# Splitting layer two's weight tiles into high and low halves in two pieces of 1024 columns

## The chip, the cores and the metric

The kernel runs on one core of one Trainium2 chip. The metric is the device time of one execution in microseconds. Three runs of the kernel before took 905.1, 906.5 and 909.17 us, with a median of 906.5 us. The profile is of one more execution.

## The reference

It is one step of a two-layer decoder trunk for 256 prompt tokens and 8 sample tokens, 264 in all, with a model width of 2048. Layer one is sliding-window attention, layer two is a gated linear recurrence (HGRN2) with 12 heads of 128 by 128 state. Each layer also has 4 memory heads, a SiLU gate as wide as the branch, one output projection, and a LayerNorm. Cut to what layer two computes:

```python
def _hgrn_branch(h, w_in, lb, norm_w, s0):
    q, f, iv, mq, g = _split(jnp.einsum('btd,de->bte', h, w_in), HG_SPLITS)
    fg = lb[None, None, :] + (1.0 - lb[None, None, :]) * jax.nn.sigmoid(f)
    qh, kh, gh, vh = silu(q), 1.0 - fg, log(fg), iv          # by heads of 128
    o, s_new = _hgrn2_chunked(qh, kh, vh, gh, s0)
    o = o * lax.rsqrt(jnp.mean(jnp.square(o), -1, keepdims=True) + RMS_EPS) * norm_w
    return o, s_new, mq, g

def _finish(h, mix, mq, g, mk, mv, w_out_i, ln_w_i, ln_b_i):
    mem_o = _mem_attend(mq, mk, mv)
    branch = jnp.concatenate([mix, mem_o], axis=-1) * jax.nn.silu(g)
    return _layer_norm(DEEPNORM_ALPHA * h + jnp.einsum('bte,ed->btd', branch, w_out_i), ln_w_i, ln_b_i)
```

## The kernel before

**A stream of tiles.** All weights and caches come through one stream of tiles of 128 rows by 2048 columns, f32 (`raw`, four buffers, loaded by SP's queue). A tile of the recurrence's state has 1024 columns. `Stream.prep` splits a tile into two f16 halves, so that f32 products can be made from f16 matmuls: line 97 has ScalarE (ACT) write the high half `hl[:, 0]`, a scaled copy; line 98 has VectorE (DVE) write the low half `hl[:, 1]`, what the copy lost. `hl` has four buffers. `Stream.parts` gives the columns of each piece: the first tile goes in four pieces, the next three in two, all others whole.

**What a tile is used for.** `proj` (line 303 to 305 by way of `passes`) multiplies a weight tile with all 264 tokens: 16 chunks of 128 rows, three matmuls for each: high by high (L303), high by the tokens' low half (L304), low by high (L305). That is 48 matmuls on TensorE (PE) for one tile. A tile of a cache or of the state needs 32 or 16 much smaller matmuls.

**The tiles of layer two**, in order: for each of six pairs of heads, two tiles for `f`, two for `hv`, two for `hq`, two of state, and for the first four pairs two for the early gates; then four for `mq`, then the memory caches (`c_mk`, four tiles, whose matmuls are named `mss`; `c_mv`, four tiles, `mso`) interleaved with the eight late gates (`g`), then the 16 tiles of the output projection (`o`).

**Work beside the stream.** The recurrence of a pair (`hg_side`) runs beside the following tiles. It makes the scores over seven levels: DVE and ACT prepare operands of level h (`prepare`: ACT high half, L1079; DVE low half, L1080; DVE's product for the next level, L1084), PE multiplies them (`hs`), and DVE masks the scores into `st` (L1111). The last level goes into `st` by ACT (L1147). Then follows a chain on PE: `pk` (transposes of the keys, L1152), `pu` (state update, L1158), `hpo` (output, L1169 to L1171) and `rms` (L1182), with steps of ACT and DVE between them. The softmax of the sample tokens over the memory keys (`mrow`, `mback`) has its own chain; it uses the same two PSUM banks (`pt`) as `pk` and `pu`, and `mso` waits for it.

**What sets the order.** The program is written unit by unit, and a scheduler puts each engine's instructions in an order of its own from that. Each engine then runs its queue strictly in that order: an instruction that waits holds all behind it.

Of the kernel before, what the change touches and what calls it, by code (L numbers as in the profile page):

```python
# [57 lines left out]
class Stream:  # L58


    def __init__(self, nc, pool, nraw, nsplit):
        self.nc, self.pool = nc, pool
        self.nraw, self.nsplit = nraw, nsplit
        self.units = []
        self.raw = {}
        self.hl = {}

    def add(self, src, fn, scale=SW, pre=None, split=True, whole=False, home=None):
        self.units.append((src, fn, scale, pre, split, split and not whole, home))
# [14 lines left out]
    def prep(self, i):  # L84
        _, _, scale, _, split, _, home = self.units[i]
        raw = self.raw[i]
        if not split:
            self.hl[i] = raw
            return
        if home:  # L90
            hl = home(i)
        else:
            hl = self.pool.tile([P, 2, 2048], F16, tag="hl", name=f"hl{i}", bufs=self.nsplit)
        for k, s in enumerate(self.parts(i)):
            if i < 4:
                self.before_split(i, k)
            hi = self.nc.scalar.activation(hl[:, 0, s], raw[:, s], AF.Copy, scale=scale)  # L97
            lo = self.nc.vector.scalar_tensor_tensor(  # L98
                hl[:, 1, s], raw[:, s], scale, hl[:, 0, s], op0=ALU.mult, op1=ALU.subtract
            )  # L100
            if i < 2:
                self.settled = hi, lo
        self.hl[i] = hl
# [31 lines left out]
def trunk_kernel(  # L135
# [42 lines left out]
    stream = Stream(nc, cp, 4, 4)  # L178
# [527 lines left out]
    def gate_unit(l, j):  # L706
        def fn(hl):
            pt = proj(hl, xhl, T, f"g{l}{j}")
            a = cp.tile([P, T], F32, tag="sil", name=f"sil{l}{j}", bufs=3)
            silu2(a, pt)  # L710
            fin[l].append((a, j))
            if len(fin[l]) >= 3:
                gate_fin(l)

        return fn
# [51 lines left out]
    def out_unit(l, i):  # L767
        def fn(hl):
            if i == 0:
                drain()  # L770
                while fin[l]:
                    gate_fin(l)
                for s in range(2):
                    acc[s] = cp.tile([P, T], F32, tag="mphl", name=f"acc{l}{s}", bufs=2)
            if l == 0 or i < NC - NSPLIT:
                out_part(l, i, hl, slice(0, T))
            else:
                held[i] = hl
                out_part(l, i, hl, slice(0, TA))
            if i == NC - 1:  # L780
                if l == 0:
                    side.append(layer_norm())
                else:
                    finish_tokens()

        return fn
# [123 lines left out]
    def wb(w, i):  # L910
        return w[i].rearrange("p c f -> p (c f)")
# [97 lines left out]
    def hq_unit(h):  # L1009
        def fn(hl):  # L1010
            p1 = H["p"]
            pt = proj(hl, xhl, T, f"hq{h}")
            if h % 2 == 0:
                cur["q"] = p1.tile([P, 2, T], F32, tag="hq", name=f"hqs{h}", bufs=2)
            silu2(cur["q"][:, h % 2], pt)
            if h % 2 == 1:
                side.append(hg_side(h // 2, cur["q"], cur["vn"], cur["fg"], cur["qk"]))

        return fn
# [31 lines left out]
    def early_gate(j):  # L1051
        def fn(hl):
            silu2(mix[:, j], proj(hl, xhl, T, f"g1{j}"))

        return fn
# [187 lines left out]
        return fn  # L1243

    state_at = {}
    for pi in range(HD // 2):
        for part, unit in (("f", f_unit), ("v", hv_unit)):
            for i in range(2):
                stream.add(wb(w_in1, NB1[part] + 2 * pi + i), unit(2 * pi + i))
        for h in (2 * pi, 2 * pi + 1):  # L1250
            stream.add(wb(w_in1, NB1["q"] + h), hq_unit(h))
            state_at[h] = len(stream.units)
            stream.add(state[pi][:, (h % 2) * TS * P : (h % 2 + 1) * TS * P], state_unit(h), SA, whole=True)
            if h < NG1:
                stream.add(wb(w_in1, NB1["g"] + h), early_gate(h))
# [9 lines left out]
    def g1(j):  # L1265
        stream.add(wb(w_in1, NB1["g"] + j), gate_unit(1, j))
# [5 lines left out]
            g1(late.popleft())  # L1272
    while late:
        g1(late.popleft())
    for i in range(NC):
        stream.add(wb(w_o[1], i), out_unit(1, i), home=hold if i >= NC - NSPLIT else None)

# [155 lines left out]
```

## Time and profile before

| what | value |
|---|---|
| runs | 905.1, 906.5, 909.17 us |
| the profiled execution's own time | 906.08 us |
| its span | 904.3 us (1.8 us lie around it) |
| PE busy | 886.6 us, 98% of the span |
| DVE busy | 701.5 us, 78% |
| ACT busy | 582.4 us, 64% |
| mean granted PE clock | 0.994 |

A matmul's end is modelled in these records, and matmuls overlap; whether PE really works is better read from the distance between their starts. Layer two's recurrence lies between about 415 and 740 us, its caches and late gates between about 730 and 800 us, and its output projection behind that.

### The profile page before, as it was taken

Reading aid. Unit: us, or ns where it says so; the run is one execution under the profiler, and the core shown is the slowest. Engines: PE = TensorE matmul, PEld = TensorE weight load, DVE = VectorE, ACT = ScalarE, POOL = GpSimd, SP = SyncE. Lnnn points to the kernel's source line nnn. Section 1 sums busy time; section 2 is a strip of 40 time slices with the busy share of each in tenths; the row PEclk is TensorE's granted clock in tenths of the full one; section 3 lists DMA queues with packets and bytes.
Section 4 is the critical chain, followed back from the end, with each engine's and each line's share of the span. In section 5 each row is a group of like instructions: output and inputs, shape, how many; then the busy total and the mean of one; then the engine's idle time right before and its main releaser. Section 6 shows DMA issues by size and latency. Waiting matters only on the chain.

```text
span 904.3 us, 21814 instructions
## 1 busy us (share of the span) xinstructions
PE 886.6 (98%) x9281; PEld 762.9 (84%) x9281; DVE 701.5 (78%) x1230; ACT 582.4 (64%) x982; POOL 34.9 (4%) x68
## 2 busy tenths in 40 slices
PE   9999999999999999999999999999999999799996
PEld 6888889678888888876888888898888888688996
DVE  6879877669886666697687887979788989678736
ACT  6767776657664444476766877777777585858415
POOL 1100010000000000002000000000000000000000
PEclk9999999999999999999999999999999999899999
DMA  9998566557785555556374655827454878456303
GB/s 340 392 353 317 188 245 209 188 208 265 262 333 192 187 192 203 207 198 214 127 292 137 216 201 174 299 101 260 160 215 164 303 283 308 172 207 244 130 2 97
DMA packets 37853, 198.67 MB, mean 220 GB/s; under 512 B 4555, under 2 KB 10732, under 8 KB 17532
## 3 DMA queue, kind: packets, MB, share of 16 engines
q1 hardware_dynamic: 33024, 181.55, 56.3%
q0 software_dynamic: 4688, 15.67, 4.6%
q8 instruction: 72, 1.18, 0.5%
q14 instruction: 25, 0.20, 0.1%
q10 hardware_dynamic: 44, 0.07, 0.0%
HBM read 180.03 MB, written 17.22 MB: 218 GB/s over the span
## 4 chain that ended last, share of the span: by engine, by line
PE 77%; DVE 8%; ACT 6%; DMA 6%; issue 3%; SPq 0%; ACTq 0%; DVEq 0%
PE o L303 5%; PE o L305 5%; PE o L304 5%; PE g L305 5%; PE g L303 5%; PE g L304 5%; DVE hl L98 4%; ACT hl L97 2%; PE hv L305 2%; PE hv L303 2%; PE hv L304 2%; DMA raw<-in_w_in 2%; PE hq L303 2%; PE hq L305 2%; PE hq L304 2%
## 5 line engine op out<-in xcount | busy, mean ns | idle before, releaser
L98 DVE SCALAR_TENSOR_TENSOR hl<-raw,hl 128x2048 f16<-128x2048 f32 (+2 forms) x168 | 358.6, 2138 | 82.0 <-ACT hl L97 81.0
L97 ACT ACTIVATE hl<-raw 128x2048 f16<-128x2048 f32 (+2 forms) x168 | 299.2, 1784 | 97.8 <-PE o L305 45.4
L305 PEld LDWEIGHTS <-hl 128*128 128x128 f16 (+2 forms) x2048 | 197.4, 98 | 31.8 <-DVE hl L98 2.9
L303 PEld LDWEIGHTS <-hl 128*128 128x128 f16 (+2 forms) x2048 | 197.3, 98 | 30.6 <-issue 2.2
L304 PEld LDWEIGHTS <-hl 128*128 128x128 f16 (+2 forms) x2048 | 197.4, 98 | 30.3 <-issue 2.2
L305 PE MATMUL g<-xhl,hl 128*128 128x264 f16 x512 | 142.0, 277 | 2.4 <-DVE hl L98 2.4
L303 PE MATMUL g<-xhl,hl 128*128 128x264 f16 x512 | 141.9, 277 | 0.0
L304 PE MATMUL g<-xhl,hl 128*128 128x264 f16 x512 | 141.9, 277 | 0.0
L303 PE MATMUL o<-mix,hl 128*128 128x264 f16 x384 | 105.4, 276 | 0.8 <-DVE xres L747 0.8
L304 PE MATMUL o<-mix,hl 128*128 128x264 f16 x384 | 105.8, 276 | 0.0
L305 PE MATMUL o<-mix,hl 128*128 128x264 f16 x384 | 105.7, 276 | 0.0
L303 PE MATMUL q<-xhl,hl 128*128 128x264 f16 x192 | 53.0, 276 | 1.0 <-DVE kst L251 1.0
L303 PE MATMUL f<-xhl,hl 128*128 128x264 f16 x192 | 52.9, 276 | 0.4 <-DVE mvhl L251 0.4
L305 PE MATMUL hv<-xhl,hl 128*128 128x264 f16 x192 | 53.0, 276 | 0.0
L303 PE MATMUL hq<-xhl,hl 128*128 128x264 f16 x192 | 53.0, 276 | 0.0
L304 PE MATMUL hq<-xhl,hl 128*128 128x264 f16 x192 | 53.0, 276 | 0.0
L305 PE MATMUL hq<-xhl,hl 128*128 128x264 f16 x192 | 53.0, 276 | 0.0
L304 PE MATMUL hv<-xhl,hl 128*128 128x264 f16 x192 | 53.0, 276 | 0.0
L303 PE MATMUL hv<-xhl,hl 128*128 128x264 f16 x192 | 53.0, 276 | 0.0
L304 PE MATMUL q<-xhl,hl 128*128 128x264 f16 x192 | 53.0, 276 | 0.0
L305 PE MATMUL q<-xhl,hl 128*128 128x264 f16 x192 | 53.0, 276 | 0.0
L304 PE MATMUL f<-xhl,hl 128*128 128x264 f16 x192 | 52.9, 276 | 0.0
(338 smaller groups left out, 1858.4 us busy)
## 6 DMA issues: line engine op xcount, KB each, us to landing
raw<-in_w_in SPq DMA_DIRECT2D x88, 1024.0 KB, 6.4
raw<-in_w_o SPq DMA_DIRECT2D x32, 1024.0 KB, 5.0
raw<-in_w_mk SPq DMA_DIRECT2D x8, 1024.0 KB, 4.9
raw<-in_w_mv SPq DMA_DIRECT2D x8, 1024.0 KB, 4.9
raw<-in_c_mk SPq DMA_DIRECT2D x8, 1024.0 KB, 5.1
raw<-in_c_mv SPq DMA_DIRECT2D x8, 1024.0 KB, 7.0
raw<-in_state SPq DMA_DIRECT2D x12, 512.0 KB, 5.4
out_ss<-raw POOLq DMA_DIRECT2D x12, 512.0 KB, 5.5
```

The source lines that it names most:

```text
L97: hi = self.nc.scalar.activation(hl[:, 0, s], raw[:, s], AF.Copy, scale=scale)
L98: lo = self.nc.vector.scalar_tensor_tensor(hl[:, 1, s], raw[:, s], scale, hl[:, 0, s], op0=ALU.mult, op1=ALU.subtract)
L303: mm(out, lhs(0), rhs(0), start=start, stop=False)
L304: mm(out, lhs(0), rhs(1), start=False, stop=False)
L305: return mm(out, lhs(1), rhs(0), start=False, stop=stop)
```

## The change

The tiles that are added to the stream between the first one of layer two's recurrence and the last gate, and that have 2048 columns, are split in two pieces of 1024 columns. Those are 64 tiles: 12 `f`, 12 `hv`, 12 `hq`, 16 gates, 4 `mq` and 8 of caches. For each, ACT writes the high half of columns 0 to 1023 and then of 1024 to 2047, and DVE writes the low halves likewise. The loads, the matmuls and the buffers stay. The tiles of state were 1024 columns wide already; the output projection's tiles stay whole.

```diff
@@ Stream.__init__
         self.hl = {}
+        self.halved = range(0)
@@ Stream.prep
-        for k, s in enumerate(self.parts(i)):
+        for k, s in enumerate((slice(0, 1024), slice(1024, 2048)) if i in self.halved else self.parts(i)):
             if i < 4:
                 self.before_split(i, k)
             hi = self.nc.scalar.activation(hl[:, 0, s], raw[:, s], AF.Copy, scale=scale)
@@ trunk_kernel
     state_at = {}
+    n_first = len(stream.units)
     for pi in range(HD // 2):
...
     while late:
         g1(late.popleft())
+    whole_w = {i for i in range(n_first, len(stream.units)) if stream.units[i][0].shape[1] == 2048}
+    stream.halved = whole_w
     for i in range(NC):
         stream.add(wb(w_o[1], i), out_unit(1, i), home=hold if i >= NC - NSPLIT else None)
```

With the pieces the scheduler also orders other work anew, on PE, DVE and ACT; the queues of SP and POOL keep their order. Up to the fourth pair the moves are of a few rows. The larger ones are around the recurrence of the last pair, among the caches and late gates. Tile numbers differ between the two programs, and so do line numbers, by one.

On ACT, at the last pair's final step into `st`, this stood before. `hl_10845` and `hl_10922` are the third and the fourth tile of `c_mv`, split whole:

```order
L97 ACTIVATE hl_10845<-raw_10579 128x2048
L733 ACTIVATE sil_10899<-g_10850 128x264
L1079 ACTIVATE qk_2_5655<-qk_10_9379 128x2x4x64
L97 ACTIVATE hl_10922<-raw_10651 128x2048
L1147 ACTIVATE st_10088<-hs_64_10507 64x4x64
L1154 ACTIVATE kn_10526<-pk_10521 128x512
L1162 ACTIVATE s_10570<-pu_10565 128x256
L672 ACTIVATE mrows_10690,mrz_10692<-mrow_10687,mrnm_10691 32x256
L1173 ACTIVATE osb_9734<-hpo_10636 128x2x256
```

And this stands there now, where `hl_10688` and `hl_10830` are the first and second tile of `c_mv`, and `hl_10762` and `hl_10909` those of gates 12 and 13:

```order
L98 ACTIVATE hl_10688<-raw_10430 128x1024 x2
L1148 ACTIVATE st_10186<-hs_64_10617 64x4x64
L730 ACTIVATE mix<-sil_10614 128x264
L734 ACTIVATE sil_10744<-g_10695 128x264
L98 ACTIVATE hl_10762<-raw_10493 128x1024 x2
L1155 ACTIVATE kn_10636<-pk_10631 128x512
L98 ACTIVATE hl_10830<-raw_10563 128x1024 x2
L1163 ACTIVATE s_10682<-pu_10677 128x256
L673 ACTIVATE mrows_10806,mrz_10808<-mrow_10803,mrnm_10807 32x256
L734 ACTIVATE sil_10886<-g_10837 128x264
L98 ACTIVATE hl_10909<-raw_10643 128x1024 x2
L1174 ACTIVATE osb_9824<-hpo_10750 128x2x256
```

The step into `st` has moved from behind `c_mv`'s fourth tile to behind its first, five tiles earlier, and splits of other tiles now lie between the steps of the chain, which followed each other before.

On PE, the chain of the last pair stood in one piece before, with no matmul of a gate in it, and `mso` of `c_mv`'s first tile right behind it:

```order
L1152 MATMUL pk_10521<-ident,qk_10_9379 128x128 x4
L1169 MATMUL hpo_10636<-st_10088,vn_9535 128x128
L1170 MATMUL hpo_10636<-st_10088,vn_9535 128x128
L1158 MATMUL pu_10565<-vn_9535,kn_10526 128x128 x4
L666 MATMUL mrow_10687<-ident,mst_10685 32x128 x2
L1171 MATMUL hpo_10636<-qk_10_9379,s_10570 128x128
L1169 MATMUL hpo_10636<-st_10088,vn_9535 128x128
L1170 MATMUL hpo_10636<-st_10088,vn_9535 128x128
L1171 MATMUL hpo_10636<-qk_10_9379,s_10570 128x128
L677 MATMUL mback_10698<-ident,mrows_10690 128x32 x2
L1182 MATMUL rms_10704<-osq_10644,ones_rms 128x264
L1182 MATMUL rms_10707<-osq_10646,ones_rms 128x264
```

Now it lies among the matmuls of two gates. Here around `pu`, where `g_10837` is gate 11:

```order
L305 LDWEIGHTS hl_10638
L305 MATMUL g_10837<-xhl,hl_10638 128x264
L306 LDWEIGHTS hl_10638
L306 MATMUL g_10837<-xhl,hl_10638 128x264
L1159 MATMUL pu_10677<-vn_9621,kn_10636 128x128 x4
L667 MATMUL mrow_10803<-ident,mst_10801 32x128 x2
L304 LDWEIGHTS hl_10638
L304 MATMUL g_10837<-xhl,hl_10638 128x264
L305 LDWEIGHTS hl_10638
L305 MATMUL g_10837<-xhl,hl_10638 128x264
```

Counted over the whole piece, between the first `hpo` and `rms` there were no matmuls of gates, and there are now 92: 30 ahead of `pu`, 22 from there to the next `hpo`, 18 from there to `mback`, and 22 from there to `rms`.

On DVE, around the scores of levels 16 and 32 of the last pair, this stood before. `hl_10714` is the second tile of `c_mv`, `hl_10791` that of gate 13; `qk_0` holds the operands of level 16, `qk_1` those of level 32:

```order
L98 SCALAR_TENSOR_TENSOR hl_10714<-raw_10453,hl_10714 128x2048
L1111 COPY_PREDICATED st_10088<-mask_t,hs_4_10290 128x32x8
L1080 TENSOR_TENSOR qk_0_5653<-qk_10_9379,qk_0_5653 128x2x16x16
L734 SCALAR_TENSOR_TENSOR sil_10768<-sil_10768,g_10719 128x264
L1111 COPY_PREDICATED st_10088<-mask_t,hs_4_10290 128x64x4
L1084 TENSOR_TENSOR qk_10_9379<-qk_10_9379,prod_10089 128x2x16x16
L98 SCALAR_TENSOR_TENSOR hl_10791<-raw_10531,hl_10791 128x2048
L1080 TENSOR_TENSOR qk_1_5654<-qk_10_9379,qk_1_5654 128x2x8x32
```

Now, where `hl_10354` is gate 9's tile and `hl_10425` the third tile of `c_mk`:

```order
L99 SCALAR_TENSOR_TENSOR hl_10354<-raw_10065,hl_10354 128x1024 x2
L1081 TENSOR_TENSOR qk_0_5661<-qk_10_9463,qk_0_5661 128x2x16x16
L1112 COPY_PREDICATED st_10186<-mask_t,hs_4_10394 128x32x8
L1085 TENSOR_TENSOR qk_10_9463<-qk_10_9463,prod_10187 128x2x16x16
L99 SCALAR_TENSOR_TENSOR hl_10425<-raw_10133,hl_10425 128x1024
L1112 COPY_PREDICATED st_10186<-mask_t,hs_4_10394 128x64x4
L99 SCALAR_TENSOR_TENSOR hl_10425<-raw_10133,hl_10425 128x1024
L1081 TENSOR_TENSOR qk_1_5662<-qk_10_9463,qk_1_5662 128x2x8x32
```

The recurrence's steps stand seven tiles earlier in DVE's queue, and a step of the recurrence lies between the two pieces of a tile. PE has `hs` of level 16 and the first matmul of level 32 next to each other now, with nothing between them, where seven matmuls of a gate lay between them before.

## The prediction

> **What bounds the kernel now.** I first read the page's head and its busy times.
>
> ```profile
> span 904.3 us, 21814 instructions
> PE 886.6 (98%) x9281; PEld 762.9 (84%) x9281; DVE 701.5 (78%) x1230; ACT 582.4 (64%) x982; POOL 34.9 (4%) x68
> ```
>
> PE is busy for 98% of the span. So only its 17.7 us of idle time can be won, and what a lowered clock costs it. Whether busy means at full rate is seen in the timeline of single matmuls. Here are three of a gate in a row, and one that waits (columns: start, duration, what, and the idle time before with what ended it):
>
> ```profile
> 762.33 0.28 PE L305 MATMUL g<-xhl,hl 128*128 128x264 f16 x1
> 762.44 0.28 PE L303 MATMUL g<-xhl,hl 128*128 128x264 f16 x1
> 762.55 0.28 PE L304 MATMUL g<-xhl,hl 128*128 128x264 f16 x1
> 763.46 0.29 PE L305 MATMUL g<-xhl,hl 128*128 128x264 f16 x1 [0.63 <-DVE hl L98]
> ```
>
> Starts are 0.11 us apart, though each record lasts 0.28 us: matmuls overlap. The last one is the first that reads a tile's low half, and waits for DVE to write it. That is the wait that pieces can shorten. Next I cut layer two into stretches (columns: stretch, length, busy time of PE, weight loads, DVE, ACT, POOL, then granted clock, share of the DMA engines, GB/s):
>
> ```profile
> 440.00:740.00 300.00, 299.69 (x3238) 265.77 (x3236) 253.18 (x485) 216.35 (x377) 9.12 (x17) 1.00 0.60 211
> 740.00:762.00 22.00, 22.00 (x274) 19.47 (x273) 22.00 (x26) 15.03 (x15) 0.00 (x0) 1.00 0.89 322
> 762.00:786.00 24.00, 18.50 (x255) 15.20 (x253) 16.70 (x29) 17.19 (x24) 0.54 (x1) 0.91 0.49 178
> 786.00:815.00 29.00, 28.70 (x245) 24.48 (x244) 22.44 (x39) 16.88 (x37) 0.00 (x0) 0.96 0.58 219
> 733.00:769.00 36.00, 35.37 (x436) 31.06 (x433) 35.93 (x40) 23.34 (x24) 0.00 (x0) 1.00 0.88 324
> ```
>
> In the recurrence (440 to 740) PE idles for 0.31 us of 300: nothing there waits for a split. All of layer two's loss lies between 762 and 815: 5.5 us idle, then 0.3, and a clock of 0.91 over 24 us and 0.96 over 29 us, which is at most 0.09 x 24 + 0.04 x 29 = 3.3 us of PE's time. Ahead of it, from 733 to 769, DVE has no gap at all (35.93 of 36), then it has 7.3 us of gaps in the 24 us in which PE idles. So the work of this part is badly spread: first DVE is full, then a chain leaves both engines waiting. The waits of PE from 740 to 815 say which (total, times, longest):
>
> ```profile
> PE g L305 <- DVE hl L98: 2.4, 2, 1.7
> PE hpo L1169 <- ACT st L1147: 1.5, 1, 1.5
> PE mback L677 <- DVE mrows L674: 1.0, 1, 1.0
> PE msc L303 <- ACT osq L1183: 0.4, 1, 0.4
> PE o L303 <- DVE xres L747: 0.3, 1, 0.3
> PE hpo L1171 <- ACT s L1162: 0.3, 1, 0.3
> ```
>
> They sum to 5.9 us. Two are waits for a low half (2.4 us). Four are links of the last pair's chain and of the softmax on its heels (1.5 + 1.0 + 0.4 + 0.3 = 3.2 us). How such a link comes about shows in the timeline of ACT and PE:
>
> ```profile
> 769.24 1.91 ACT L97 ACTIVATE hl<-raw 128x2048 f16<-128x2048 f32 x1 [3.84 <-issue]
> 771.06 0.36 ACT L1147 ACTIVATE st<-hs 64x256 f32<-64x256 f32 x1
> 769.31 0.63 PE L1152 MATMUL pk<-ident,qk 128*128 128x128 f32 x4
> 771.47 0.49 PE L1169 MATMUL hpo<-st,vn 128*128 128x128 f32 x2 [1.53 <-ACT st L1147]
> ```
>
> PE has nothing but the chain left in its queue, and the step that it needs stands on ACT behind a split of 1.91 us.
>
> **The change, part by part: the pieces.** The trace has splits of both sizes, and neighbours that give their spacing.
>
> ```profile
> L98 DVE SCALAR_TENSOR_TENSOR hl<-raw,hl 128x2048 f16<-128x2048 f32 x146 | 333.9, 2291 | 73.9 <-ACT hl L97 73.2
> L98 DVE SCALAR_TENSOR_TENSOR hl<-raw,hl 128x1024 f16<-128x1024 f32 x18 | 22.0, 1220 | 3.4 <-ACT hl L97 3.1
> L97 ACT ACTIVATE hl<-raw 128x2048 f16<-128x2048 f32 x146 | 277.8, 1906 | 92.2 <-PE o L305 45.4 <-DMA raw<-in_w_in 11.5 <-PE mv L593 10.2
> L97 ACT ACTIVATE hl<-raw 128x1024 f16<-128x1024 f32 x18 | 18.9, 1051 | 2.6 <-DMA raw<-in_w_kv 2.6
> 682.68 1.22 DVE L98 SCALAR_TENSOR_TENSOR hl<-raw,hl 128x1024 f16<-128x1024 f32 x1
> 683.82 0.69 DVE L1084 TENSOR_TENSOR qk<-qk,prod 128x512 f32<-128x512 f32 x1
> 754.49 4.50 DVE L98 SCALAR_TENSOR_TENSOR hl<-raw,hl 128x2048 f16<-128x2048 f32 x2
> ```
>
> By durations a tile in two pieces costs DVE 2 x 1220 - 2291 = 149 ns more, and ACT 2 x 1051 - 1906 = 196 ns. By spacing it is less on DVE: a piece takes 683.82 - 682.68 = 1.14 us of the queue, a whole tile 4.50 - 2.29 = 2.21 us, so 0.07 us more. For 64 tiles DVE is busy for 4.5 to 9.5 us more, ACT for at most 12.5 us. Of these tiles 44 lie in the recurrence (12 `f`, 12 `hv`, 12 `hq`, 8 gates): at most 6.6 us on a DVE with 46.8 us of gaps there, under a PE that never waits. I take 0; without that cover it would be 3 to 6.6 us.
>
> In return the first low half exists sooner: ACT 1051 ns and DVE 1220 ns, 2.27 us, in place of 1906 + 2291 = 4.20 us. Where DVE is the later one, the first piece ends 2291 - 1220 = 1.07 us earlier. Of the two waits for a low half, the one above (0.63 us) goes, and the other (1.7 us) loses 1.07: **-1.7 us**, if DVE's queue is no later.
>
> A sentence of the Trainium skill bears on that. Trace Analysis, in "Optimizing Scalar/DVE Operations", says that larger operations help where Scalar or Vector is saturated, and that breaking up instructions may help where it isn't and yet causes bubbles. By the first half the gates' 20 tiles would only cost here, 1.4 to 3.0 us, since DVE is full from 733 to 769; by the second, 1.7 us are won. The trace has both cases within 50 us, so the order decides.
>
> **The order.** The step into `st` moves five tiles ahead on ACT, and on PE 92 matmuls of gates come to lie within the chain, 10.3 us at 0.112 us each: 30 before `pu`, 22 before the second `hpo`, 18 before `mback`, 22 before `rms`. Every link has at least 18 x 0.112 = 2.0 us of cover, where the longest wait was 1.5 us. **-3.2 us**. What is late next is the first gate behind it: its split stands behind `rms`, two table loads and the exponentials on ACT. Against that, the `mso` of `c_mv`'s tiles release their `hl` buffers earlier, and whole gates lie in between.
>
> To be covered, the chain must begin earlier, and so the recurrence's steps stand seven tiles earlier in DVE's queue, in the stretch in which it is full. Their cost:
>
> ```profile
> L1080 DVE TENSOR_TENSOR qk<-qk,qk 128x512 f16<-128x512 f32 x42 | 29.2, 695 | 9.3 <-ACT qk L1079 9.2
> L1084 DVE TENSOR_TENSOR qk<-qk,prod 128x512 f32<-128x512 f32 x36 | 24.8, 689 | 0.4
> L1111 DVE COPY_PREDICATED st<-mask_t,hs 128x256 f32<-128x256 int32 x36 | 19.1, 531 | 0.6 <-PE hs L305 0.5
> ```
>
> At level 32, PE's first `hs` needs only ACT's high half. Then 27 matmuls of gate 9 follow, 3.0 us. In that time DVE has to do two pieces, one mask and the low half, 1.22 + 0.53 + 1.22 + 0.70 = 3.7 us, and it begins while ACT still makes the high half, about 0.6 us. It is nearly even: each such level can cost from 0 to some 0.7 us, three of them 0 to 2. With the gate behind `rms`, new waits are bounded by 0 and by what DVE has in gaps to lose, 7 us. I take **+1.0 us**, near the even count.
>
> **The clock.** It falls where PE idles, and I let it keep a quarter of its 3.3 us: **-2.5 us**.
>
> ```profile
> 786.00:788.00 2.00, 2.00 (x11) 1.36 (x10) 2.00 (x1) 2.00 (x6) 0.00 (x0) 0.50 0.64 201
> ```
>
> Here PE is busy at a clock of 0.50, 11 matmuls in 2 us, just after its idle stretch. TensorE: Matmul & The Clock Gate, of the Trainium skill, in "What's actually happening", has the gate halve the clock after an idle window of about 3.4 us; the value 0.50 agrees. By that rule a chain without long idle time would give back all 3.3 us, and the sum would be 0.8 us lower.
>
> **The sum**: -1.7 - 3.2 + 1.0 - 2.5 = -6.4 us. The profiled execution took 906.08 us (span 904.3 and 1.8 around it), which gives 899.7 us. The median of the three runs is 0.4 us above that execution; I forecast **900 us**, and count the cases in the same terms.
>
> **Rivals.**
> 1. All is won: the waits and the clock, 5.9 + 3.3 = 9.2 us, so 897 us. For it: after the change DVE has 20 x 0.15 = 3 us more to do in a part that holds 14 us of its gaps (762 to 815). Against it: the DMA engines are at 0.88 in the full stretch.
> 2. DVE stays the bound: PE's waits move from the chain to low halves and keep their size, and the 20 tiles add 1.4 to 3.0 us: 908 to 910 us, no difference that can be told (0.5%, 4.5 us, is about what a measurement of this kernel tells from no change). For it: 35.93 of 36. This is the first half of the skill's rule above as a mechanism of this kernel; the trace bears it out for 36 us only.
> 3. Slower: DVE paces PE through all of 733 to 815. Its extra 3.0 us land on PE, which then stops often enough to have the clock of 0.91 for 82 us, 7.4 us in place of 3.3. Together 7.1 us: 913.6 us. It decides from where DVE's gaps of 7.3 and 6.6 us are not reached by the work put forward, that is, if PE arrives at every low half first. Against it: the chain is in front of the gates in every queue.
> 4. The pieces change no order that matters, and only the two waits shrink: 904.8 us. The program's order speaks against it.
>
> **Chances.** The forecast, 897.5 to 902.5 us: 0.50. Rival 1: 0.12. Rivals 2 and 4: 0.28. Rival 3: 0.10. Faster by over 0.5% (below 902) takes nearly all of the first two: 0.60. Within 0.5%: 0.30. Slower: 0.10. The range for 8 in 10 reaches from just under rival 1 to rival 2's near end: 896 to 908 us.
>
> **What would show it.** Right: PE idle under 2 us between 762 and 786, the chain's `hpo` and `mback` gone from PE's waits, a clock of 1.00 there, and 440 to 740 as it was. Splits of 1024 at 1.22 and 1.05 us, 128 on each engine more. Wrong: waits of PE for `hl` L98 above 4 us in total, `hs` among PE's waits, or DVE full past 769. If the recurrence before 740 grows by over 1 us, my zero there is wrong.

## The result, and the profile after

Over 12 runs each, the kernel before took 906.42 us (median) and the changed kernel 900.07 us (898.57 to 903.36). The ratio is 0.993, with a 95% interval of 0.9917 to 0.9943. The forecast was 900 us. The profiled execution of the changed kernel took 900.73 us.

Here are the head of its page and its busy times:

```profile
span 898.9 us, 21938 instructions
PE 884.6 (98%) x9281; PEld 761.1 (85%) x9281; DVE 703.3 (78%) x1294; ACT 587.7 (65%) x1046; POOL 34.9 (4%) x68
```

PE's share is the same 98%. DVE is busy for 1.8 us more and ACT for 5.3 us, with 64 instructions more on each, where the prediction had 4.5 to 9.5 us and at most 12.5 us. The span is 5.4 us shorter. The stretches say where (columns as before: length, busy time of PE, weight loads, DVE, ACT, POOL, then granted clock, DMA share, GB/s):

```profile
440.00:740.00 300.00, 297.66 (x3226) 263.06 (x3224) 255.83 (x538) 219.95 (x424) 9.12 (x17) 1.00 0.57 211
740.00:762.00 22.00, 22.00 (x287) 19.81 (x284) 22.00 (x32) 15.14 (x22) 0.00 (x0) 1.00 0.82 304
762.00:786.00 24.00, 23.87 (x308) 20.74 (x307) 18.82 (x35) 23.16 (x39) 0.54 (x1) 1.00 0.66 244
786.00:815.00 29.00, 28.17 (x248) 24.15 (x246) 23.01 (x36) 18.37 (x31) 0.00 (x0) 1.00 0.58 218
733.00:769.00 36.00, 35.71 (x454) 31.45 (x452) 32.59 (x49) 26.98 (x41) 0.54 (x1) 1.00 0.75 276
```

Between 762 and 786 PE now idles for 0.13 us in place of 5.5, and the clock is 1.00 in both late stretches. But the recurrence, 440 to 740, has 2.34 us of idle time where it had 0.31. PE's waits from 740 to 904, and then from 415 to 740:

```profile
PE o L304 <- DVE xres L748: 1.8, 1, 1.8
PE o L304 <- ACT mix L730: 0.5, 1, 0.5
PE mpo L305 <- DVE mphl L252: 0.2, 1, 0.2
```

```profile
PE hs L304 <- ACT qk L1080: 2.3, 7, 0.4
```

Of the waits that were listed for 740 to 815, the two for a low half and the four of the chain are gone. New are seven waits of `hs`, six of them in the recurrence. The output projection's waits for `xres`, 0.3 and 0.5 us in the kernel before, are now one of 1.8 us. (Line numbers are one higher in the changed kernel: L98 is now ACT's split, L99 DVE's.)

To see what each stage won or lost, I take the starts of three kinds of matmuls from the two timelines of PE: the first `f`, the last `hq` and the last `o` of a held tile.

| stage | before | after | difference |
|---|---|---|---|
| start to first `f` | 420.09 | 419.14 | -0.95 |
| first `f` to last `hq` (recurrence) | 281.64 | 284.39 | +2.75 |
| last `hq` to last `o` (gates, output) | 191.41 | 184.25 | -7.16 |
| from there to the end | 11.16 | 11.12 | -0.04 |
| span | 904.3 | 898.9 | -5.4 |

So the forecast came out right with a term that was wrong: the recurrence, which I had at 0, lost 2.75 us. Two of the signs that I had named for being wrong are there: `hs` among PE's waits, and a recurrence longer by over 1 us.

### The profile page after: what moved, and what is told of

The parts are those of the page before. It is cut to its first block, busy times and chain, and to the rows that moved or that the text cites. A ratio compares the mean times of both kernels' runs of the same rounds, so it can differ in the third digit from the quotient of the medians.

```text
span 898.9 us, 21938 instructions
## 1 busy us (share of the span) xinstructions
PE 884.6 (98%) x9281; PEld 761.1 (85%) x9281; DVE 703.3 (78%) x1294; ACT 587.7 (65%) x1046; POOL 34.9 (4%) x68
## 4 chain that ended last, share of the span: by engine, by line
PE 81%; DVE 11%; ACT 4%; issue 2%; DMA 1%; ACTq 0%; DVEq 0%
PE o L304 5%; PE o L306 5%; PE o L305 5%; PE g L304 5%; PE g L306 5%; PE g L305 5%; DVE hl L99 5%; PE q L304 2%; PE q L306 2%; PE q L305 2%; PE hv L304 2%; PE hv L306 2%; PE hv L305 2%; PE hq L305 2%; PE hq L304 2%
## 5 line engine op out<-in xcount | busy, mean ns | idle before, releaser
L99 DVE SCALAR_TENSOR_TENSOR hl<-raw,hl 128x1024 f16<-128x1024 f32 (+2 forms) x232 | 365.0, 1592 | 68.4 <-ACT hl L98 68.0
L98 ACT ACTIVATE hl<-raw 128x1024 f16<-128x1024 f32 (+2 forms) x232 | 305.0, 1344 | 87.8 <-PE o L306 47.0
```

Of the source, the lines that this page charges most:

```text
L99: lo = self.nc.vector.scalar_tensor_tensor(hl[:, 1, s], raw[:, s], scale, hl[:, 0, s], op0=ALU.mult, op1=ALU.subtract)
```

## The experiments

**Two theories.** The order: a tile in pieces acts through the place that the scheduler then gives to other steps. In the gates part the last pair's chain comes to stand between gates; in the recurrence some steps come to stand behind pieces. The pieces: shorter splits are what gains, each where it is. The table shows where the chain stands in TensorE's program order in each kernel: how many gate tiles are still to come when `pk` begins, how many gate matmuls lie between each of its steps and the `hs` or step ahead of it, and what each trace shows. The idle time and the time at a granted clock of 0.50 are those of PE from 762 to 815 us. What the low clock cost is an estimate: half of the time at 0.50 in which PE was busy with anything but `mso`, since `mso`'s matmuls start as close together at 0.50 as at 1.00 (see the last section). The last column is the stage from the last `hq` to the last `o`.

| kernel | split in pieces | tiles left at `pk` | gate matmuls ahead of `pk` / first `hpo` / `pu` / second `hpo` / `mback` | idle, us | at 0.50, us | its cost (estimate), us | last `hq` to last `o`, us |
|---|---|---|---|---|---|---|---|
| before | none | 2.0 | 0 / 0 / 0 / 0 / 0 | 5.8 | 6.8 | 2.7 | 191.4 |
| late8 | 8 late gates | 2.0 | 0 / 0 / 0 / 0 / 0 | 5.7 | 6.8 | 3.0 | 192.1 |
| caches12 | mq, caches | 2.4 | 0 / 18 / 0 / 0 / 0 | 5.8 | 6.8 | 2.6 | 191.4 |
| gates20 | gates part | 2.4 | 27 / 7 / 12 / 0 / 0 | 5.1 | 13.7 | 4.8 | 192.6 |
| rec44 | recurrence | 3.6 | 33 / 20 / 2 / 22 / 34 | 4.0 | 6.8 | 1.7 | 186.6 |
| last6 | last pair | 3.6 | 33 / 20 / 2 / 22 / 34 | 3.8 | 10.2 | 3.2 | 187.7 |
| changed | both, 64 | 5.0 | 19 / 0 / 30 / 22 / 18 | 1.0 | 0 | 0 | 184.3 |
| from5 | last pair and gates part | 5.0 | 19 / 0 / 30 / 22 / 18 | 1.0 | 0 | 0 | 183.3 |
| all_urgent | both, 64, other order | 2.0 | 0 / 0 / 0 / 0 / 0 | 5.8 | 6.8 | 2.6 | 190.8 |

The waits go with these places. That of `hpo` for `st` stands only where no gate lies ahead of `pk` or of the first `hpo` (before, late8, all_urgent). That for `s` stands only where none lies ahead of the second `hpo`. That of `mback` stands in before, late8 and all_urgent; in caches12 and gates20 `rms` comes ahead of it and waits 1.1 us for `osq` instead.

The edits change only which tiles `stream.halved` holds, unless said otherwise.

**gates20.** The recurrence is whole.

```diff
+    n_gates = len(stream.units)          # ahead of the mq tiles
-    whole_w = {i for i in range(n_first, len(stream.units)) if ...}
+    whole_w = {i for i in range(n_gates, len(stream.units)) if ...}
```

> Only the 20 tiles of the gates part (mq, both caches, late gates) are split in two pieces; the 44 of the recurrence are whole. Theory 1 (order): the pieces act by the place that they give the last pair's chain on TensorE, and in the recurrence by the place of DVE's qk steps behind two pieces. Here the chain stands with only 7 gate matmuls (0.8 us) ahead of its first hpo and none ahead of its second hpo and of mback, so part of the chain's 3.2 us and of the clock's loss stays in 762 to 815; the recurrence's hs waits (3.0 us after the change) are gone. 900 to 903 us. Theory 2 (pieces): the gain of 9.5 us in the gates part comes from the smaller pieces there and stays whole, and the recurrence costs nothing: 896 to 898 us.

Measured: 906.76 us, ratio 1.000 (0.999 to 1.0011). Neither theory had that. Pieces in the gates part alone win nothing, so the theory of the pieces falls. But the order's forecast, 900 to 903, was also too good by about 4 us. The waits of PE from 740 to 815, and its stretches:

```profile
PE g L304 <- DVE sil L735: 2.5, 1, 2.5
PE hpo L1172 <- ACT s L1163: 1.3, 1, 1.3
PE rms L1183 <- ACT osq L1178: 1.1, 1, 1.1
```

```profile
762.00:786.00 24.00, 21.61 (x255) 17.54 (x253) 17.15 (x31) 17.73 (x33) 0.55 (x1) 0.74 0.54 197
774.00:776.00 2.00, 2.00 (x4) 1.13 (x4) 0.15 (x1) 1.97 (x3) 0.54 (x1) 0.50 0.81 238
```

The two waits for a low half are gone and the chain's waits are fewer, as the place of its steps would have it; a wait for `sil` is new. That wait I had not foreseen, nor how long the clock would stay low: after the waits for `s` and `osq` (1.3 and 1.1 us, PE busy for 1.61 of the 4 us from 770 to 774) it stood at 0.50 from 773.4 to 787.1. By the estimate that cost 4.8 us, where it was 2.7 us before.

**rec44.** The gates part is whole.

```diff
-    whole_w = {i for i in range(n_first, len(stream.units)) if ...}
+    whole_w = {i for i in range(n_first, n_gates) if ...}
```

> Only the 44 tiles of the recurrence are split in two pieces; mq, caches and late gates are whole. Theory 1 (order): on TensorE the last pair's chain stands between gate matmuls here too (20 ahead of the first hpo, 22 ahead of the second, 31 ahead of rms), so its 3.2 us of waits and most of the clock's 3.3 us go although no tile there is in pieces; the recurrence costs its 2.7 us: 901 to 905 us, with no wait of hpo on st. Theory 2 (pieces): what gained is the smaller pieces in the gates part, and they are gone: the time before plus 2.7 us, 908 to 910 us.

Measured: 904.89 us, ratio 0.9978 (0.9964 to 0.9993), at the end of the order's range and clear of the 908 of the other theory. Its trace is of an execution that took 902.62 us, faster than most of its runs. PE's waits from 740 to 815:

```profile
PE msc L304 <- ACT ms L615: 3.8, 1, 3.8
PE mso L697 <- DVE msphl L252: 0.2, 1, 0.2
```

No tile in the gates part is in pieces, and yet the waits for `st`, `mrows` and the low halves are gone: pieces in the recurrence moved them. In their place stands a single wait of the memory softmax on ACT. The recurrence takes 284.38 us, as in the changed kernel (284.39).

**late8** and **caches12**: of the gates part only the 8 late gates, or only the other 12.

```diff
-    stream.halved = whole_w
+    stream.halved = set(late_at)          # late_at: the units that g1 adds
```

> Only the 8 late gates are split in two pieces. Theory 1 (order): on TensorE the last pair's chain stands in one piece, as before the change, so its 3.2 us of waits and the lowered clock stay; only the waits for a gate's low half (2.4 us) shrink by up to 1.7 us: 903.5 to 906.5 us. Theory 2 (pieces): the gates were what waited, and in pieces they win most of the 9.5 us: 897 to 900 us.

> Only mq and the caches (12 tiles) are split in two pieces; late gates and recurrence are whole. Theory 1 (order): 18 gate matmuls (2.0 us) stand ahead of the first hpo, whose wait of 1.5 us goes; the rest of the chain stands in one piece and waits; so 1.5 us and a part of the clock's 3.3 us are won: 901 to 905 us. Theory 2 (pieces): the late gates are whole and keep their waits of 2.4 us, and the caches' tiles had none: 905 to 907 us, no change.

Measured: late8 906.4 us (1.0007, 0.9993 to 1.0021); caches12 904.81 us (0.9978, 0.9967 to 0.9989). Both lie in the range of the theory of the order; late8 is far from the 897 to 900 of the other theory, and caches12 only just outside its 905 to 907. In caches12 the wait for `st` is gone as expected, and PE waits for other steps: 2.0 us (`mso` for `msphl`), 1.4 (`msc` for `osq`), 1.1 (`rms`) and 0.9 (`hpo` for `s`). Its trace, of a run of 905.77 us, shows no gain in the gates part; where the 1.5 us of its median come from stays open. In late8 the gates that waited are in pieces, and PE waits much as before:

```profile
PE g L306 <- DVE hl L99: 2.0, 1, 2.0
PE mback L678 <- DVE mrows L675: 1.0, 1, 1.0
PE hpo L1170 <- ACT st L1148: 0.7, 1, 0.7
```

There is one wait for a low half in place of two, 2.0 us in place of 2.4, but the longest has grown from 1.7 to 2.0 us, though the first piece does come as early as counted. DVE's row there:

```profile
782.05 2.35 DVE L99 SCALAR_TENSOR_TENSOR hl<-raw,hl 128x1024 f16<-128x1024 f32 x2
```

PE resumes at 783.33, with the first piece, where a whole split from 782.05 would have ended at 784.34. It only came to the wait sooner: the gate's first matmul, right behind `mso`, starts at 780.98 us, where it was 783.32. What is won there is gone by the end: the clock is at 0.50 as long as before, and PE waits 0.5 us for `ms` in addition. With the chain in its old place, the pieces' own effect is worth nothing in the total.

**from5** and **last6** split the question further. In both, pairs 0 to 4 are whole; last6 has the gates part whole too.

```diff
     for pi in range(HD // 2):
+        if pi == 5:
+            n_from = len(stream.units)
...
+    whole_w = {i for i in range(n_from, len(stream.units)) if ...}      # last6: range(n_from, n_gates)
```

> Split in two pieces are the last pair's 6 tiles (f, hv, hq) and the 20 of the gates part; the 38 tiles of pairs 0 to 4 are whole. Each engine's order from the last pair's f tiles to the end is that of the changed kernel. Theory 1 (order): the gates part gains as in the changed kernel, and the recurrence's hs waits (2.7 us) are gone: 896.5 to 898.5 us. Rival: the pieces of all pairs carry the gain together, or the recurrence's loss is given back behind it, where PE would only arrive earlier at the output's transfers: 899 to 901 us, or, if only the 6 tiles' share is won, above 904 us.

> Only the last pair's 6 tiles (f, hv, hq) are split in two pieces; the gates part's 20 are whole, as in the kernel with 44 tiles in pieces, and each engine's order in the gates part is that kernel's. Theory 1 (order): its time less the recurrence's 2.7 us: 901.5 to 903 us; msc still waits for ms some 3.8 us. The four kernels then make a square: nothing split 906.4, gates part alone 906.8, last pair alone 902, both 897.5. Rival (the recurrence's pieces cost by themselves, or each tile's pieces bring a share of their own): 904 to 906 us.

Measured: from5 898.39 us (0.9909, 0.9895 to 0.9922), last6 901.82 us (0.9953, 0.9941 to 0.9966). Both as the theory of the order had it. The four kernels without pieces in pairs 0 to 4 make a square: nothing 906.4, gates part alone 906.8 (from another chip, where the kernel before took 906.35), last pair alone 901.8, both 898.4. Pieces in the gates part are worth nothing alone and 3.4 us once the last pair's chain has moved. Why they are worth something there shows in last6's ACT and PE:

```profile
773.39 1.89 ACT L98 ACTIVATE hl<-raw 128x2048 f16<-128x2048 f32 x1
775.19 0.22 ACT L250 ACTIVATE msphl<-mback 128x64 f16<-128x64 f32 x1
```

```profile
772.94 0.27 PE L306 MATMUL msc<-mkhl,mqhl 128*128 128x256 f16 x1
776.98 0.37 PE L304 MATMUL msc<-mkhl,mqhl 128*128 128x256 f16 x1 [3.76 <-ACT ms L615]
```

A whole split of 1.89 us stands ahead of the softmax's steps, and PE has nothing else left: 3.76 us of idle time, and by the estimate 3.2 us of clock behind it. In from5 the recurrence is as before and the gates part as in the changed kernel:

```profile
440.00:740.00 300.00, 299.59 (x3268) 265.73 (x3267) 258.39 (x508) 219.37 (x396) 9.11 (x17) 1.00 0.60 213
762.00:815.00 53.00, 52.04 (x553) 44.84 (x551) 42.54 (x68) 41.47 (x67) 0.00 (x0) 1.00 0.63 223
```

**all_urgent** has all 64 tiles in pieces and another order.

```diff
+    def urgent(gen, n):
+        while True:
+            with tc.high_priority(n):
+                try:
+                    next(gen)
+                except StopIteration:
+                    return
+            yield
...
-                side.append(hg_side(h // 2, cur["q"], cur["vn"], cur["fg"], cur["qk"]))
+                hg = hg_side(h // 2, cur["q"], cur["vn"], cur["fg"], cur["qk"])
+                side.append(urgent(hg, 400))
```

> All 64 tiles are split in two pieces as in the changed kernel; in addition the steps of every pair's recurrence have a higher priority for the scheduler, and in the order that comes out the last pair's chain stands on TensorE in one piece with no gate between its steps, as before the change. Theory 1 (order): the chain waits again, 3 to 5 us with the clock's loss; the hs waits in the recurrence shrink, as in two of the four pairs the low-half steps stand ahead of the pieces again: 904 to 908 us. Theory 2 (pieces): the pieces are what gains, and the time stays at 900 us or below.

Measured: 908.16 us, ratio 1.0019 (1.0011 to 1.0028): the same 64 tiles in pieces, and 8 us over the changed kernel. The chain's waits of before the change are all back, as are the 6.8 us at a clock of 0.50, and low halves are waited for. The theory of the pieces, at 900 us or below, falls; the time is just over the 904 to 908 of the order:

```profile
PE g L306 <- DVE hl L99: 2.0, 1, 2.0
PE hpo L1180 <- ACT st L1158: 1.5, 1, 1.5
PE mback L678 <- DVE mrows L675: 1.0, 1, 1.0
```

One part of the expectation failed: the recurrence's `hs` waits did not shrink. They are 2.3 us in three pieces, 0.8 us at the longest, with one in each of three pairs where the changed kernel has two. This higher priority is no cure for them.

**from5_held** adds the last 8 output tiles.

```diff
+    stream.halved |= set(range(len(stream.units) - NSPLIT, len(stream.units)))
```

> As the kernel with the last pair and the gates part in pieces, and also the last 8 tiles of the output projection (held) in two pieces. There DVE's step into xres (L748), which frees a PSUM bank for TensorE, stood behind a whole split of 2.29 us and made TensorE wait 1.8 us in the changed kernel. If the wait is that of one engine's queue, it falls to 0.7 us or less and the time by 1 to 1.5 us against the same kernel with whole held tiles: 895.5 to 897.5 us. Rival: the transfers of w_o set the pace there, and nothing is won.

Measured: 897.19 us (0.9901, 0.9886 to 0.9915) beside from5's 898.39, with overlapping runs (895.3 to 899.4 and 897.12 to 899.1). The wait for `xres` is gone from its trace (0.9 us in from5's), but it is also absent from the second trace of the changed kernel, where the held tiles are whole. Whether time is won stays open here. Its trace is of its slowest run, 899.4 us, and shows a limit of such readings: ACT's and DVE's orders in the recurrence are those of from5, and yet `hs` waits for 0.8 us in two pieces, at 535 and 541 us, where from5's two traces have at most 0.2. ACT had waited 1.90 us for a tile's transfer just before, and split it late:

```profile
529.84 1.91 ACT L98 ACTIVATE hl<-raw 128x2048 f16<-128x2048 f32 x1 [1.90 <-DMA raw<-in_w_in]
```

So a wait of `hs` in a single trace need not come from the order. The changed kernel has its seven at the same steps in both of its traces.

**The last four ran together on one chip**: the changed kernel and from5 again, from3, and one with all that looked useful ("best").

```diff
-        if pi == 5:                       # from3
+        if pi == 3:
...
+    stream.halved |= set(range(len(stream.units) - NSPLIT, len(stream.units)))      # best: from5 and these
+    stream.halved |= set(range(n_first, n_first + 2))
```

> The changed kernel once more, beside the three that follow: 900 us, as before.

> The kernel with the last pair and the gates part in pieces once more, on the same chip as the changed kernel. Theory: 1.5 to 2.5 us below the changed kernel (2.7 us of the recurrence less 0.6 us for the wait ahead of the first f tile, which only the changed kernel is without): 897.5 to 898.5 us. Rival: the difference was chance, and both stand within 0.7 us.

> Tiles of the pairs 3, 4 and 5 and of the gates part in pieces, 12 more than in the kernel that starts with pair 5. In DVE's queue the low-half step of level 4 stands behind three pieces and two masks in the chains of pairs 2 and 3, where the changed kernel waits about 1.0 us for each of the pairs 1, 2 and 3. Theory (each such place costs 1.0 us): PE's hs waits at about 575 to 586 and 629 to 640 us, none at 521 to 532, and 2.0 us over the kernel that starts with pair 5: 900 to 900.8 us. Rival (the pieces' own busy time costs, 0.07 to 0.15 us a tile): 1.2 to 2.7 us more, spread over the pairs and with no such waits; second rival: no difference.

> The last pair, the gates part, the last 8 output tiles and the first two f tiles in pieces. Theory: against the kernel with the last pair and the gates part alone, the wait of 0.8 us between the last mv and the first f goes (as in the changed kernel) and the 1.1 us in which TensorE waits for xres: 1.5 to 2 us less, 896 to 897 us. Rival: what is won ahead is given back at the output's transfers: within 0.5 us of it.

| kernel | median, us | lowest to highest | ratio to before, 95% interval |
|---|---|---|---|
| changed | 899.85 | 898.77 to 902.24 | 0.9931 (0.9913 to 0.9949) |
| from5 | 897.16 | 896.37 to 900.73 | 0.9901 (0.9882 to 0.9919) |
| from3 | 900.01 | 898.68 to 901.68 | 0.9928 (0.9912 to 0.9944) |
| best | 897.11 | 896.83 to 898.32 | 0.9898 (0.988 to 0.9915) |

The medians of from5 and of the changed kernel differ by 2.7 us here, and by 1.7 us in the earlier runs, which were not made side by side; both times from5 is the faster. The expectation was 1.5 to 2.5. In from3 the waits lie where its order has them, none between 510 and 560, and from 570 to 650:

```profile
PE hs L304 <- ACT qk L1080: 1.4, 3, 0.7
```

Their starts lie 0.84, 0.45 and 0.56 us too far apart, at 585, 629 and 639 us, together 1.85; the recurrence takes 283.50 us where from5's first trace has 281.70. That speaks against the pieces' own busy time, which would be spread over the tiles of the pairs 3 and 4.

"best" was to win 1.5 to 2 us over from5 and wins nothing that can be told, as its rival had it. Its trace lacks the wait for `xres`, but the wait ahead of the first `f` is still there (0.8 us between starts): two tiles in pieces did not move that. So from5, with 26 tiles in pieces in place of 64, is the version to keep.

## Why the prediction was right, and where it was not

**"Two waits for a low half, -1.7."** Both went, 2.4 us. The pieces of the gates aren't needed for that: rec44 lost them too, with whole gates. The effect that I had in mind, an earlier first piece, is there in late8 and doesn't shorten the time.

**"The chain, -3.2."** Right in size, and the order is the cause. The four links are gone in the changed kernel and in from5, and back in all_urgent, which has the same pieces and no gates within the chain. Whether it is the gates on PE or the earlier steps on ACT and DVE was not tried apart: the scheduler moved them together.

**"+1.0 for new waits."** Near in size, wrong in place. Neither `hs` at level 32 nor the gate behind `rms` waits much. From 762 to 815 PE still idles for 0.13 + 0.83 us, for `mix` and `mphl` at the end of the gates. A further 1.8 us for `xres`, in place of 0.5 behind 815 us, came in the output projection in this execution. In the second profiled execution of the changed kernel it is absent, and the span is 897.6 us.

**"The clock, -2.5."** All of it came back: 1.00 in both stretches. But the whole was not 3.3 us, which was an upper bound; by the estimate in the table it was 2.7. So -2.5 was nearly right because a bound that was too high and a share that was too low cancel. By the rule of the Trainium skill's TensorE: Matmul & The Clock Gate, "What's actually happening", the clock is lowered after an idle window of about 3.4 us. The changed kernel agrees: no such window, and 1.00. gates20 does not: there the clock fell after waits of 1.3 and 1.1 us.

**"Of these tiles 44 lie in the recurrence ... I take 0."** This step failed, at +2.75 us. I argued from busy time (6.6 us under 46.8 us of gaps, and a PE that never waits) and did not look at the order there as I did in the gates part. DVE's queue at level 4 of pair 1 in the changed kernel:

```profile
526.07 1.22 DVE L99 SCALAR_TENSOR_TENSOR hl<-raw,hl 128x1024 f16<-128x1024 f32 x1
527.21 0.73 DVE L1112 COPY_PREDICATED st<-mask_t,hs 128x256 f32<-128x256 int32 x1
527.72 1.26 DVE L99 SCALAR_TENSOR_TENSOR hl<-raw,hl 128x1024 f16<-128x1024 f32 x1
528.89 0.72 DVE L1112 COPY_PREDICATED st<-mask_t,hs 128x256 f32<-128x256 int32 x1
529.41 1.26 DVE L99 SCALAR_TENSOR_TENSOR hl<-raw,hl 128x1024 f16<-128x1024 f32 x1
530.58 0.68 DVE L1081 TENSOR_TENSOR qk<-qk,qk 128x512 f16<-128x512 f32 x1
```

The same place in from5, with whole tiles:

```profile
525.56 2.29 DVE L99 SCALAR_TENSOR_TENSOR hl<-raw,hl 128x2048 f16<-128x2048 f32 x1
527.76 0.69 DVE L1081 TENSOR_TENSOR qk<-qk,qk 128x512 f16<-128x512 f32 x1
528.37 0.72 DVE L1112 COPY_PREDICATED st<-mask_t,hs 128x256 f32<-128x256 int32 x1
```

With whole tiles the low half of level 4 (L1081) stands behind one split and ahead of the masks. With pieces, three of them and both masks go first, since a piece fits where a whole split didn't. ACT's next high half then starts at 532.02, in from5 at 531.84; counted from each kernel's first `f` (419.14 and 420.02) it is 112.88 and 111.82, 1.06 us later. PE has used up its lead by then:

```profile
532.03 0.28 PE L306 MATMUL hv<-xhl,hl 128*128 128x264 f16 x1
532.70 0.20 PE L304 MATMUL hs<-qk 128*128 128x64 f16 x1 [0.40 <-ACT qk L1080]
```

The starts lie 0.56 us further apart than two matmuls of this kind do; with 0.45 at 521 that is 1.0 us for the pair, and 3.0 us for the pairs 1, 2 and 3. That pieces in these pairs bring it is shown by from5 and from3. That it is the place of L1081 is read from the timelines, agrees with the lateness, and is the same in both traces of the changed kernel. It wasn't tried alone, and all_urgent has waits of this size at other steps.

**What I missed at the start**: the first `f` waited in the kernel before (the row below, of its waits from 415 to 740), and doesn't in the changed kernel. That is 0.6 of the first stage's 0.95 us; the other 0.35 us lie in the start of the execution, where both programs are alike.

```profile
PE f L303 <- DVE mvhl L251: 0.4, 1, 0.4
```

**The rivals.** That DVE stays the bound fell: DVE isn't full from 733 to 769 any more (32.59 us of 36), and from 762 to 815 it is busier than before. That the pieces change no order that matters is refuted by all_urgent. That all is won came true in the gates part (5.8 us of idle time and some 2.7 of clock went down to 1.0), and the recurrence and `xres` gave 2.75 and 1.3 us of it back. The total was right because these errors cancel. That it came within 0.1 us is luck.

## What to carry to other kernels

Where a scheduler sets the order, a change of granularity is a change of order, and has to be read stage by stage from the new order. Covered busy time proves nothing for a stage in which a chain of small steps shares the queues with the pieces. An edit that is worth nothing at one place alone (906.8) may be worth 3.4 us once the same edit at another place has moved the work, so try edits in pairs ahead of dropping them. And the least set that brings the order wanted, here 26 tiles of 64, kept the gain and dropped the loss.

## What the runs showed of the hardware that was not expected

The lowered clock came in steps, and it did not slow every matmul. In each trace the clock stands at 0.50 for a whole multiple of 3.41 us: 6.83 us in the kernel before (two stretches of 3.41 us with as much at 1.00 between them) and in late8, caches12, rec44 and all_urgent, 10.24 us in last6, 13.65 us in gates20. These rows are from 2 us slices of gates20:

```profile
772.00:774.00 2.00, 0.86 (x9) 0.67 (x7) 1.96 (x6) 1.67 (x5) 0.01 (x1) 0.86 0.00 0
780.00:782.00 2.00, 2.00 (x81) 2.00 (x79) 1.77 (x6) 2.00 (x3) 0.00 (x0) 0.50 0.03 8
784.00:786.00 2.00, 2.00 (x11) 1.36 (x10) 1.96 (x4) 2.00 (x6) 0.00 (x0) 0.50 0.73 238
798.00:800.00 2.00, 2.00 (x20) 1.75 (x19) 2.00 (x7) 0.60 (x2) 0.00 (x0) 1.00 0.51 180
```

From 784 to 786, 11 matmuls of a gate lie in 2 us; from 798 to 800, at a clock of 1.00, there are 20 of gates and of `mpo`. The 81 from 780 to 782 are all of `mso`, some 0.026 us apart, and at 1.00 it is 0.025. So time at 0.50 is not yet time lost. These rows are of last6:

```profile
774.00:776.00 2.00, 0.00 (x0) 0.10 (x1) 2.00 (x6) 2.00 (x5) 0.00 (x0) 1.00 0.00 0
782.00:784.00 2.00, 2.00 (x35) 1.81 (x33) 2.00 (x3) 2.00 (x2) 0.00 (x0) 0.50 0.03 8
```

In last6 a wait of 3.8 us was followed by 10.24 us at 0.50, which cost 3.2 us by the estimate; the same wait in rec44 was followed by 6.83 us, which cost 1.7. In gates20 no single wait ahead of the fall was longer than 1.3 us (2.4 us idle within 4), and the low clock lasted longest and cost most, 4.8 us. So the length of one wait does not tell what the clock will cost. What sets the number of steps stays open.
